# Which queue issues the last stores, and one unit's channel sums four steps later, in a streaming encoder layer

## The chip, the cores and the metric

The kernel runs on one core of a Trainium2 chip. TensorE (PE in the profile) multiplies matrices, with its weight loads shown as PEld; VectorE (DVE), ScalarE (ACT) and GpSimd (POOL) compute on vectors, and SyncE (SP) only issues transfers. SP, ACT and POOL can each issue DMA transfers from their own queue; an instruction in such a queue waits until the one before it has been issued. The metric is the device time of one execution in microseconds.

## The reference

One layer of an encoder processes 512 new frames of one stream (prompt) and 64 frames of a running stream (sample) with 512 cached frames. Everything is float32:

```python
proj = rmsnorm(x, g_norm1) @ w_in               # 2048 -> 6144
q, k, v, gb, gc, hc = split(proj)               # 6 x 1024
q = rmsnorm(q by head, g_q); k = rmsnorm(k by head, g_k)   # 8 heads x 128
o_attn = stick_breaking(q, k, v)                # causal attention
o_conv = gb * conv3_causal(gc * hc)
x = x + concat(rmsnorm(o_attn), rmsnorm(o_conv)) @ w_out
h2 = rmsnorm(x, g_norm2)
x = x + (silu(h2 @ w_gate) * (h2 @ w_up)) @ w_down   # hidden width 5632
```

It returns x for both streams, and the new rows of k, v and of the convolution's state. The two streams are processed together as 576 columns (frames), in two halves of 288; the first half holds prompt frames 0 to 287, the second prompt frames 288 to 511 and the 64 sample frames.

## The kernel before

Each large product is cut into units. A unit is a 256 x 256-blocked strip of weights times the frames, done as a two-by-two block product with seven multiplications in place of eight (numbered 1 to 7 in the code, `run(n, p_)`); each float32 operand is split into a high and a low part, and three matmuls make one full product. A whole multiplication has eight groups of three matmuls. Between groups, `pipe.tick()` counts one **step**, and work that was spawned with a delay is put into the program when its step comes. A unit yields four output blocks, called (c, i): c is the column block of 128 channels, i the half of the frames.

The kernel's stages are: the input stage with the first projection units (to about 100 us), the rest of the input projection (units -22 to -1, to about 570 us), attention and the output projection with it (to about 855 us), gate and up units, and down units, of which the last ones are issued between 1800 us and the end. The order of PE's instructions is written out everywhere. In the down stage the order on ACT, DVE, SP and POOL is written out too (`manual_schedule`); in the projection stage a planner orders these four engines, following what PE's order and the data allow.

**Channel sums.** A unit of kind "qk" gives a head's queries (c = 0) and keys (c = 1). When a block is finished, `a_done` (lines 885 to 907) adds and scales it into a tile E, squares it, and splits the squares into a high and a low part, `s2` (lines 903, 904 on ACT, 905 on DVE). It then spawns `normed` (line 844). That waits a number of steps and issues two matmuls with a matrix of ones, `channel_sums` (lines 283 and 284: the high part, then the low part), four activations on ACT (849 to 852) and three vector operations, and when both halves are done a store of the tile on SP. Key tiles go on to `tokens`, which transposes and stores them. The second qk unit is unit -18 (4 - NA, where NA is 22): the fifth in the list of input units. Its four blocks finish after the multiplications 2, 5, 3 and 4, so `normed` runs four times for it.

**The last stores.** Finished blocks of the down stage are stored in one of two ways. For all units but the last, `store_blocks` transposes a block on DVE (line 1607) and stores it from SP in four pieces (line 1613), with two more for the sample frames if the block is of the second half (line 1615). For the last unit, `store_y` transposes on PE (line 1644), copies with ACT (lines 1647 and 1653), and then stores: a block of the first half by one transfer from SP (line 1656) and one from POOL; a block of the second half by a 64 KB transfer from SP (line 1635), a 48 KB and a 16 KB transfer of the next 128 frames (lines 1635 and 1637) and one from POOL. The last unit's blocks finish in the order (0,0), (1,1), (1,0), (0,1).

The framework that builds the program gives the transfers of SP and ACT eight completion counters, handed out in one rotation over both queues in the order in which its planner places the transfers. A transfer waits on its queue until the counter's last holder has landed. POOL's transfers have eight counters of their own.

Of the kernel before, what the change touches and what calls it, by code (L numbers as in the profile page):

```python
# [16 lines left out]
P = 128  # L17
# [41 lines left out]
NA = len(HEADS_A)  # L59
# [43 lines left out]
def tile_hybrid_stream_step(  # L103
# [6 lines left out]
    nc = tc.nc  # L110
# [30 lines left out]
    def misc(name):  # L141
        return ps_z.tile([P, 512], F32, tag="misc", name=name, bufs=2)
# [13 lines left out]
    NU = len(gu)  # L156
# [110 lines left out]
    def col(name, i=0):  # L267
        return vec[:, rows[name] + i : rows[name] + i + 1]
# [12 lines left out]
    def channel_sums(src_hi, src_lo, a, b, name):  # L281
        ps = misc(name)[:, : b - a]
        mm(ps, oner, src_hi, start=True, stop=False)
        mm(ps, oner, src_lo, start=False, stop=True)
        return ps
# [343 lines left out]
    def hl_tile(name):  # L629
        return tmp.tile([P, 2, HALF], F32, tag="hl", name=name, bufs=3).rearrange("p i t -> p (i t)")  # L630
# [211 lines left out]
        return ((a, min(b, TP), 0),) + (((TP, b, 2),) if b > TP else ())  # L842

    def normed(n, h, c, a, b, s2, E):
        yield 12 if n == -2 else 20
        ms = ss = channel_sums(s2[:, 0], s2[:, 1], a, b, "ss")
        yt = hl_tile("yt")
        y, t = yt[:, :HALF], yt[:, HALF:]
        nc.scalar.activation(out=ms, in_=ss, func=AF.Identity, scale=1.0 / P, bias=epsc)
        nc.scalar.activation(out=y, in_=ms, func=AF.Ln)  # L850
        nc.scalar.activation(out=y, in_=y, func=AF.Exp, scale=-0.5)
        nc.scalar.activation(out=t, in_=y, func=AF.Square)
        nc.vector.scalar_tensor_tensor(out=t, in0=t, scalar=-0.5, in1=ms, op0=ALU.mult, op1=ALU.mult)
        nc.vector.scalar_tensor_tensor(out=t, in0=t, scalar=1.5, in1=y, op0=ALU.add, op1=ALU.mult)
        nc.vector.scalar_tensor_tensor(out=E[:, a:b], in0=E[:, a:b], scalar=col("gk") if c else gqs, in1=t,
                                       op0=ALU.mult, op1=ALU.mult)
        seen[n, c] = seen.get((n, c), 0) + 1
        if seen[n, c] == 2:
            nc.sync.dma_start(out=qk_dram[h, c], in_=E)
            if c:  # L860
                pipe.spawn((last_tokens if n == -2 else tokens)(E, kp[:, h, :], ks[:, h, :], None, 11 if n == -2 else 20))
# [25 lines left out]
    def a_done(n, c, i, ps, part):  # L887
        kind, g = UNITS[n][:2]
        a, b = HALVES[i]
        if kind in ("v", "qk"):  # L890
            if (n, c) not in etile:
                etile[n, c] = (lpool.tile([P, UW - 2], F32, tag=f"c{n + 2}", name="E2")[:, :T]
                               if n > -3 and c == 0 else e_tile(f"E{n}"))
            E = etile[n, c]
            bank = ps
            if part is not None:
                nc.vector.tensor_tensor(out=E[:, a:b], in0=ps, in1=part, op=ALU.add)
                ps = E[:, a:b]
            nc.vector.tensor_tensor(out=E[:, a:b], in0=ps, in1=R1[:, a:b], op=ALU.mult)
            if kind == "qk":  # L900
                sq = hl_tile("sq")[:, :HALF] if c == i == 1 else bank
                s2 = tmp.tile([P, 2, HALF], F32R, tag="hl", name="s2", bufs=3)
                nc.scalar.activation(out=sq, in_=E[:, a:b], func=AF.Square)
                nc.scalar.copy(out=s2[:, 0], in_=sq)
                nc.vector.tensor_tensor(out=s2[:, 1], in0=sq, in1=s2[:, 0].bitcast(F32), op=ALU.subtract)
                pipe.spawn(normed(n, g, c, a, b, s2, E))
                return
            seen[n, c] = seen.get((n, c), 0) + 1
            if seen[n, c] == 2:
                h = 2 * g + c  # L910
                pipe.spawn((last_tokens if n == -1 else tokens)(E, vp[:, h, :], vs[:, h, :], v_dram[h], 3 if n == -1 else 7))
            return
# [631 lines left out]
    for d, v in visits.items():  # L1544
        n = next(a for a, b in zip(v, v[1:]) if a >= NGU + 10 and b >= a + 4)
# [51 lines left out]
    def store_blocks(n, c, i):  # L1597
        d = UNITS[n][1]
        src, c0, f0 = acc[d, c, i], (2 * d + c) * P, HALVES[i][0]
        n_p = min(HALF, TP - f0)  # L1600

        def work():
            yield 9
            if not spare:
                spare.extend(down["pool"].tile([P, HALF], F32, tag=f"ob{k}", name="ob") for k in range(2))
            ob = spare.pop(0)
            nc.vector.transpose(out=ob, in_=src)
            spare.append(src)
            yield 5
            for k in range(P // BK):  # L1610
                rows = ob[k * BK : (k + 1) * BK, :n_p].rearrange("j (t c) -> j t c", c=BK)
                cg = slice(c0 + k * BK, c0 + (k + 1) * BK)
                nc.sync.dma_start(out=yp[f0 : f0 + n_p, cg].rearrange("(t j) c -> j t c", j=BK), in_=rows)
            for a in range(n_p, HALF, BK):
                nc.sync.dma_start(out=ys[a - n_p : a - n_p + BK, c0 : c0 + P].rearrange("j (g c) -> g j c", c=BK),
                                  in_=ob[:, a : a + BK])

        pipe.spawn(work())
# [3 lines left out]
    def store_y(n, c, i):  # L1622
        if n < NU - 1:
            store_blocks(n, c, i)
            return

        d = UNITS[n][1]
        src, cs, f0 = acc[d, c, i], slice((2 * d + c) * P, (2 * d + c + 1) * P), HALVES[i][0]
        r = HALF - 2 * P

        def put(f, ap, queue=nc.sync):

            rows, n_p = ap.shape[0], max(min(TP - f, ap.shape[0]), 0)
            if n_p:
                queue.dma_start(out=yp[f : f + n_p, cs], in_=ap[:n_p])
            if n_p < rows:
                queue.dma_start(out=ys[f + n_p - TP : f + rows - TP, cs], in_=ap[n_p:])

        def work():
            yield 9  # L1640
            po = misc("pot")[:, : 3 * P]
            for q in range(3):
                w = min(P, HALF - q * P)
                nc.tensor.transpose(po[:w, q * P : (q + 1) * P], src[:, q * P : q * P + w], ident)
            yield 3
            ob = src[:, : 2 * P].rearrange("p (i c) -> p i c", c=P)
            nc.scalar.copy(out=ob, in_=po[:, : 2 * P].rearrange("p (i c) -> p i c", c=P))
            if len(rests) % 2 == 0:
                rests.append(spare.pop(0))
            else:  # L1650
                rests.append(rests[-1])
            obs = rests[-1][:r, : P] if len(rests) % 2 else rests[-1][:r, P : 2 * P]
            nc.scalar.copy(out=obs, in_=po[:r, 2 * P :])
            yield 4
            if i == 0:
                nc.sync.dma_start(out=yp[: 2 * P, cs].rearrange("(i p) c -> p i c", p=P), in_=ob)
            else:
                put(f0, ob[:, 0, :])
                put(f0 + P, ob[:, 1, :], nc.scalar if n == NU - 1 else nc.sync)
            put(f0 + 2 * P, obs, nc.gpsimd if n == NU - 1 else nc.sync)  # L1660

        pipe.spawn(work())


# [80 lines left out]
```

## Time and profile before

| | |
|---|---|
| median of three runs | 2339.37 us (2337.11 to 2339.61) |
| the profiled execution | 2339.12 us |
| its span, first to last instruction | 2337.4 us |
| PE busy | 2316.1 us, 99% of the span |
| DVE, ACT, POOL busy | 84%, 52%, 13% |
| DMA | 368.58 MB, mean 158 GB/s |
| granted PE clock, mean | 0.998 |

A row of a timeline gives the start, the duration, the engine, the line of the kernel, the operation and what it writes and reads; "x4" means four merged instructions, and brackets give idle time of the engine before it with what ended it. An engine's name with a q is its queue (SPq, ACTq): there the issue of a transfer is shown, not the transfer. A row of waits says who waited for whom, and gives total time, number of times and the longest.

### The profile page before, as it was taken

What the parts mean: (1) busy time and instruction counts of PE and PEld (TensorE: products, weight loads), DVE (VectorE), ACT (ScalarE), POOL (GpSimd) and SP (SyncE); (2) the same over time, 40 slices, a digit from 0 to 9 for tenths busy, and PEclk for the clock granted to TensorE, in tenths of its full rate; (3) what the DMA queues carried; (4) which work ended last, traced back from release to release, by engine and by line L of the source; (5) the groups of instructions that cost most, each with busy time, mean ns of one, the idle gap of its engine ahead of it and who ended that gap; (6) DMA issues with size and microseconds to landing.
All of it is one profiled execution on the core that took longest, in us unless ns stands there. A gap on an engine that the chain in (4) does not pass through costs nothing.

```text
span 2337.4 us, 43553 instructions
## 1 busy us (share of the span) xinstructions
PE 2316.1 (99%) x17432; PEld 2306.9 (99%) x17432; DVE 1954.1 (84%) x2871; ACT 1221.6 (52%) x2170; POOL 300.6 (13%) x374
## 2 busy tenths in 40 slices
PE   9999999999999999999999999999999999999997
PEld 9999999999999999999999999999999999999997
DVE  8889989897777898888888888888888778887896
ACT  8556656456877654444444444444444444444443
POOL 0211121110332320000000000000000002431222
PEclk9999999999999999999999999999999999999999
DMA  8434343546743454543444444444444936875653
GB/s 271 139 113 129 91 142 110 142 134 206 197 137 118 163 190 126 159 152 121 154 142 136 154 129 149 143 139 150 130 148 140 361 115 225 227 217 188 208 133 80
DMA packets 533771, 368.58 MB, mean 158 GB/s; under 512 B 70278, under 2 KB 518016, under 8 KB 533568
## 3 DMA queue, kind: packets, MB, share of 16 engines
q1 hardware_dynamic: 526752, 356.32, 48.7%
q0 software_dynamic: 6384, 9.21, 2.2%
q8 instruction: 136, 2.23, 0.4%
q14 instruction: 67, 0.55, 0.1%
q10 hardware_dynamic: 432, 0.27, 0.0%
HBM read 285.52 MB, written 80.23 MB: 156 GB/s over the span
## 4 chain that ended last, share of the span: by engine, by line
PE 92%; DVE 3%; ACT 3%; DMA 1%; issue 1%; POOL 0%; SPq 0%; POOLq 0%; DVEq 0%; ACTq 0%
PE psy L405 45%; PE psw L405 23%; PE psx L405 11%; PE pjo L224 6%; PE pj L691 1%; PE pjz L691 1%; DVE whl L229 1%; PE psv L405 1%; PE pjm L691 1%; DMA raw_a<-in_w_down_dram 0%; ACT ph L228 0%; PE psx L556 0%; ACT whi L176 0%; DMA raw_b<-in_w_down_dram 0%; PE z L1176 0%
## 5 line engine op out<-in xcount | busy, mean ns | idle before, releaser
L229 DVE TENSOR_TENSOR whl<-raw_a,whl 128x1024 fp32r<-128x1024 f32 (+4 forms) x384 | 432.2, 1126 | 54.8 <-ACT whl L228 53.4
L405 PE MATMUL psy<-t,whl 128*128 128x288 f32 x3000 | 447.0, 294 | 0.0
L228 ACT CAST whl<-raw_a 128x1024 fp32r<-128x1024 f32 (+4 forms) x384 | 360.1, 939 | 141.5 <-PE psx L405 46.7
L405 PE MATMUL psy<-h_s,whl 128*128 128x288 f32 x2766 | 416.5, 294 | 0.6 <-ACT part L428 0.6
L405 PEld LDWEIGHTS psy<-t,whl 128*128 128x128 f32 x3000 | 414.3, 188 | 0.0
L405 PE MATMUL psw<-t,whl 128*128 128x288 f32 x2688 | 388.9, 294 | 0.0
L405 PEld LDWEIGHTS psy<-h_s,whl 128*128 128x128 f32 x2766 | 383.1, 188 | 0.9 <-ACT part L428 0.8
L405 PEld LDWEIGHTS psw<-t,whl 128*128 128x128 f32 x2688 | 366.8, 188 | 0.0
L228 ACT CAST whl<-raw_b 128x1024 fp32r<-128x1024 f32 (+5 forms) x234 | 211.3, 905 | 208.1 <-issue 71.6
L229 DVE TENSOR_TENSOR whl<-raw_b,whl 128x1024 fp32r<-128x1024 f32 (+5 forms) x234 | 254.7, 1089 | 74.0 <-ACT whl L228 72.6
L428 ACT COPY part<-psy 128x288 f32<-128x288 f32 x309 | 123.1, 399 | 343.3 <-PE psy L405 340.9
L405 PE MATMUL psx<-h_s,whl 128*128 128x288 f32 x1164 | 170.2, 294 | 0.0
L405 PEld LDWEIGHTS psx<-h_s,whl 128*128 128x128 f32 x1164 | 159.6, 188 | 0.0
L228 ACT CAST whl<-s 128x1024 fp32r<-128x1024 f32 (+5 forms) x103 | 95.3, 925 | 122.6 <-PE psw L405 115.0
L405 PE MATMUL psy<-t12a,whl 128*128 128x288 f32 x1056 | 150.6, 295 | 0.4 <-ACT part L428 0.4
L405 PE MATMUL psw<-t34a,whl 128*128 128x288 f32 x1056 | 150.6, 295 | 0.0
L405 PEld LDWEIGHTS psy<-t12a,whl 128*128 128x128 f32 x1056 | 143.5, 188 | 0.9 <-ACT part L428 0.7
L405 PEld LDWEIGHTS psw<-t34a,whl 128*128 128x128 f32 x1056 | 143.3, 188 | 0.0
L1454 POOL DMA_DIRECT2D hid_dram<-form x7 | 5.2, 739 | 952.1 <-DVE form L229 944.9
L229 DVE TENSOR_TENSOR whl<-s,whl 128x1024 fp32r<-128x1024 f32 (+5 forms) x103 | 110.3, 1071 | 19.9 <-ACT whl L228 19.3
L224 PE MATMUL pjo<-mixc,whi 128*128 128x288 f32 x512 | 119.0, 300 | 0.0
L224 PE MATMUL pjo<-mixa,whi 128*128 128x288 f32 x512 | 102.8, 296 | 0.0
(565 smaller groups left out, 3920.6 us busy)
## 6 DMA issues: line engine op xcount, KB each, us to landing
hid_dram<-form SPq DMA_DIRECT2D x147, 288.0 KB
raw_a<-in_w_in_dram SPq DMA_DIRECT2D x22, 1024.0 KB
raw_b<-in_w_in_dram SPq DMA_DIRECT2D x22, 1024.0 KB
raw_b<-in_w_gate_dram SPq DMA_DIRECT2D x22, 1024.0 KB
raw_b<-in_w_up_dram SPq DMA_DIRECT2D x22, 1024.0 KB
raw_a<-in_w_gate_dram SPq DMA_DIRECT2D x22, 1024.0 KB
raw_a<-in_w_up_dram SPq DMA_DIRECT2D x22, 1024.0 KB
h_s<-hid_dram SPq DMA_DIRECT2D x10, 2016.0 KB
```

The lines of the kernel that those rows point to most:

```text
L224: mm(ps, w_[:, k, csl], x_[:, a:b], start=(k == 0 and n == 0), stop=(k == nk - 1 and n == 2))
L228: cast = nc.scalar.copy(out=hi, in_=src)
L229: (lo_eng or nc.vector).tensor_tensor(out=lo, in0=src, in1=hi.bitcast(F32), op=ALU.subtract)
L405: mm(ps, whl[:, w_, j, :], x_, start=(start and j == 0 and q == 0), stop=(j == len(xs_) - 1 and q == 2), skip_group_check=True)
L428: nc.scalar.copy(out=t, in_=st["y"])
L691: mm(banks_[c][i], w3[:, kt % 8, c * P : (c + 1) * P], t[:, x_, :], start=(kt == 0 and n == 0), stop=(kt == KD - 1 and n == 2))
L1454: q.dma_start(out=hid_dram[fp][2 * n - 2 : 2 * n].rearrange("f p t -> p f t"), in_=t.bitcast(F32))
```

## The change

Two edits. The first takes ACT out of the last unit's stores: the second `put` of a second-half block loses its queue argument and takes the default, SP. It is called for blocks (1,1) and (0,1), and each call makes two transfers (48 KB and 16 KB). The second lets the generator `normed` of unit -18 wait 24 steps instead of 20; all other qk units keep 20, and unit -2 keeps 12.

```diff
     def normed(n, h, c, a, b, s2, E):
-        yield 12 if n == -2 else 20
+        yield 12 if n == -2 else 24 if n == 4 - NA else 20
         ms = ss = channel_sums(s2[:, 0], s2[:, 1], a, b, "ss")
...
             else:
                 put(f0, ob[:, 0, :])
-                put(f0 + P, ob[:, 1, :], nc.scalar if n == NU - 1 else nc.sync)
+                put(f0 + P, ob[:, 1, :])
             put(f0 + 2 * P, obs, nc.gpsimd if n == NU - 1 else nc.sync)
```

## The prediction

> **What bounds the kernel now.** I read the page's busy times first, then PE's waits, then the busy time by stretch at the end, then SP's queue there instruction by instruction.
>
> ```profile
> span 2337.4 us, 43553 instructions
> PE 2316.1 (99%) x17432; PEld 2306.9 (99%) x17432; DVE 1954.1 (84%) x2871; ACT 1221.6 (52%) x2170; POOL 300.6 (13%) x374
> ...
> L229 DVE TENSOR_TENSOR whl<-raw_a,whl 128x1024 fp32r<-128x1024 f32 (+4 forms) x384 | 432.2, 1126 | 54.8 <-ACT whl L228 53.4
> ```
>
> ```profile
> PE psx L556 <- DMA xin<-in_x_prompt_dram: 4.0, 2, 3.7
> ...
> PE psy L405 <- ACT part L428: 1.0, 2, 0.6
> PE ss L284 <- DVE s L905: 0.7, 1, 0.7
> ```
>
> PE is busy for all but 21.3 us of the span. PE's waits (total us, times, longest; the row of line 229, a weight split, is needed below) explain few of these, and one of them is the operation that the second edit moves: line 284, the second matmul of a channel sum. The rest lies at the end:
>
> ```profile
> 2314.20:2325.40 11.20, 9.98 (x76) 9.39 (x75) 4.81 (x10) 3.56 (x11) 3.87 (x5) 1.00 0.05 11
> 2325.40:2337.40 12.00, 0.00 (x0) 0.00 (x0) 0.00 (x0) 0.26 (x2) 1.00 (x2) 0.60 0.36 77
> ```
>
> The columns are length, busy PE, PEld, DVE, ACT, POOL, granted clock, DMA share, GB/s. After 2325.4 the core computes nothing and stores for 12.0 us; in the 11.2 us before that, with results at hand, the DMA engines are 5% busy. SP's queue says why (start, us, instruction):
>
> ```profile
> 2314.12 0.32 SPq L1613 DMA_DIRECT2D out_dram<-acc  x1
> 2325.43 0.32 SPq L1613 DMA_DIRECT2D out_dram<-acc  x1
> ...
> 2326.78 1.13 SPq L1615 DMA_DIRECT2D out_dram<-acc  x2
> 2328.01 1.97 SPq L1613 DMA_DIRECT2D out_dram<-acc  x4
> ...
> 2331.26 1.90 SPq L1613 DMA_DIRECT2D out_dram<-acc  x4
> 2333.26 0.40 SPq L1656 DMA_DIRECT2D out_dram<-acc  x1
> ...
> 2334.27 0.40 SPq L1656 DMA_DIRECT2D out_dram<-acc  x1
> 2334.76 0.42 SPq L1635 DMA_DIRECT2D out_dram<-acc  x1
> SPq L1613 <- DMA out_dram<-acc: 11.2, 2, 11.0
> ```
>
> SP issues the first store of a block at 2314.12 and the second at 2325.43: it waited 11.0 us for a transfer to out_dram. All later stores queue behind it, and the last leaves at 2334.76. So SP's queue, not PE, sets the end.
>
> Whose transfer was it? SP had issued none since 2314.12. The others:
>
> ```profile
> 2323.40 0.37 ACT L1647 COPY acc<-pot 128x256 f32<-128x256 f32 x1 [2.69 <-PE pot L1644]
> ...
> 2323.80 0.34 ACTq L1635 DMA_DIRECT2D out_dram<-acc  x1
> 2324.18 0.44 ACTq L1637 DMA_DIRECT2D out_dram<-acc  x1
> 2324.71 0.37 ACT L1647 COPY acc<-pot 128x256 f32<-128x256 f32 x1 [0.79 <-PE pot L1644]
> ...
> 2325.14 0.36 ACT L1647 COPY acc<-pot 128x256 f32<-128x256 f32 x1
> ...
> 2321.11 0.57 POOL L1635 DMA_DIRECT2D out_dram<-acc  x1
> 2324.22 0.52 POOL L1637 DMA_DIRECT2D out_dram<-acc  x1 [2.55 <-ACT acc L1653]
> 2326.10 0.50 POOL L1637 DMA_DIRECT2D out_dram<-acc  x1
> DMA to landing us min/median/max: 1.7/2.3/2.8
> ```
>
> The last row is the time from issue to landing of line 1635's GpSimd stores. By it GpSimd's store of 2321.11 has landed by 2323.9, and that of 2324.22 not before 2325.9: neither fits 2325.43. ACT's of 2323.80 fits, at 1.6 us. The program says the same: SP's and ACT's transfers take eight completion counters in one rotation, each waiting until its counter's last holder has landed, and SP's stuck store comes next after ACT's first store on that counter. ACT could not issue that one before its block was copied, at 2323.77; so a store whose data had lain ready since about 2314.1 waited for the end of the computation.
>
> **The change, part by part.**
>
> *No store on ACT.* Four stores leave ACT's queue, two for each of the blocks (1,1) and (0,1), and SP gets four. With only SP on the counters, each waits for SP's own transfer eight places back. Eight issues at 0.49 us (2334.27 to 2334.76) are 3.9 us, more than the longest landing above, 2.8 us, so I cost that wait at nothing; a landing beyond 3.9 us would show.
>
> From 2314.12 on, worked out from the intervals of the same queue when it ran freely. A block of six stores takes 2331.26 - 2328.01 = 3.25 us, one of four 2333.26 - 2331.26 = 2.00 us. The data of the last two come from
>
> ```profile
> 2316.01 0.47 DVE L1607 STREAM_TRANSPOSE acc<-acc 128x288 f32<-128x288 f32 x1
> 2318.16 0.47 DVE L1607 STREAM_TRANSPOSE acc<-acc 128x288 f32<-128x288 f32 x1
> ```
>
> so the stuck block ends at 2314.12 + 3.25 = 2317.37, the next at 2320.62, the last at 2322.62; their data are ready at 2316.48 and 2318.63, before their turns. The store of (0,0), ready before GpSimd's at 2321.11, goes at 2322.62 and SP is free at about 2323.12. The next three, of (1,1), wait for the copy that ends at 2323.77. So SP idles 0.7 us: that is the cover of the 16 issues from 2314.6 on, and what they take beyond 0.04 us more each goes to the end. From 2323.80, where ACT started, seven stores follow at 0.50 us: three of (1,1), one of (1,0), three of (0,1), the last at 2326.80. The data of (1,0) (2325.08) and (0,1) (2325.50) are ready ahead of 2325.30 and 2325.80 even by the old times; with ACT's two issues (2323.80 to 2324.62) gone from between its copies, the copy of 2324.71 can come some 0.4 us earlier, but SP's rate hides that. GpSimd keeps its stores. SP's last issue moves from 2334.76 to 2326.80: **-7.96 us**.
>
> What then follows the last issue:
>
> ```profile
> L1741 SPq DRAIN  x3: 7/7/7, 2336.6 to 2336.9; - x3
> L1741 POOLq DRAIN  x3: 40/93/3136, 2326.1 to 2337.1; - x3
> ```
>
> Now 2337.4 - 2334.76 = 2.64 us, kept. GpSimd's own ending is next in line: its drain starts at 2326.1, takes at most 3.14 us, and the closing barrier 0.8 us (2336.6 to 2337.4), so at the old times it would hold the end at 2330.0, and at 2329.4 if its stores come 0.6 us sooner behind an ACT that no longer issues. SP's sum, 2326.80 + 2.64 = 2329.44, stands between. Bounds for this part: -8.3 us (a last transfer of 16 KB that lands 0.3 us sooner than one of 64 KB; an estimate) to -6.7 (all 16 issues at the slowest step of the free stretch, (2328.01 - 2326.78)/2 = 0.62 us: 16 x 0.125 = 2.0 us, less the 0.7 of cover, 1.3; GpSimd's 2330.0 lies inside). I take -7.96, since its terms are intervals of this queue itself.
>
> The Trainium skill, page "DMA: Bandwidth & Descriptors", section "Issuing engines are not separate DMA queues", says that transfers of all issuing engines share the same 16 DMA engines, and that issuing from several saves only the sequencer's time to issue. By that rule alone the change gives up 4 x 0.49 = 1.96 us of saved issuing and wins nothing. No bandwidth is lost or won here, but the rule does not count a completion counter shared between two queues; the 11.0 us row does.
>
> *One unit's channel sums four steps later.* A step is three matmuls. The unit is -18, the second with queries and keys; each of its four sums moves by 12 matmuls.
>
> ```profile
> 177.30 0.45 DVE L905 TENSOR_TENSOR s<-psx,s 128x288 fp32r<-128x288 f32 x1
> 176.78 0.29 PE L283 MATMUL ss<-s,oner 128*128 128x288 f32 x1
> 177.80 0.40 PE L284 MATMUL ss<-s,oner 128*128 128x288 f32 x1 [0.72 <-DVE s L905]
> 178.04 1.35 PE L405 MATMUL psy<-t12a,whl 128*128 128x288 f32 x9
> 179.23 3.37 PE L405 MATMUL psy<-b,whl 128*128 128x288 f32 x24
> ...
> 187.59 0.29 PE L283 MATMUL ss<-s,oner 128*128 128x288 f32 x1
> ...
> 187.85 1.38 PE L405 MATMUL psw<-t34a,whl 128*128 128x288 f32 x9
> ```
>
> The undisturbed sum takes 187.85 - 187.59 = 0.26 us of PE's time, this one 178.04 - 176.78 = 1.26: 1.00 us lost, waiting for the low half, which is there at 177.75. Moved, the sum starts after the product's last nine matmuls, 179.23 - 178.04 = 1.19 us later, at 177.97: 0.2 us to spare. Gain 1.00 us. The other three sums did not wait and cost the same elsewhere. But all four now fall on the end of a product; at two of these ends (products 5 and 6) ACT must also copy the bank that the product after next writes, and the sum's chain on ACT may get ahead of the copy. The nearest row is the wait of line 405 for such a copy, 0.6 us at the longest: twice, 1.2. So this part lies between -1.0 and +0.2; I take **-0.9**, near the end where ACT, which is half idle, takes the copy in time. What is queued behind: the unit's query and key rows go to SP's queue 1.6 us later, and so may weight loads behind them; the waits show no wait of PE for any DMA after the first inputs, and weight splits run four products of 24 matmuls ahead, at 0.13 us a matmul (nine in 1.19) 12.7 us, so nothing is charged. Buffers of the sums' rotating tiles are held 1.6 us longer, covered by the same lead.
>
> **Sum.** 2337.4 - 7.96 - 0.9 = 2328.5 us of span. The profiled run took 2339.12, 1.72 outside the span and 0.25 below the median of 2339.37. 2328.5 + 1.72 + 0.25 = 2330.5.
>
> **Rivals.**
> - *The shift buys nothing, or a copy waits at a product's end* (the second part at 0 to +0.2, with SP's slip of up to 1.3 us beside it): 2331.4 to 2332.9. For it: only 0.2 us to spare.
> - *SP's queue becomes slow*: SP is bound by its issues from 2314 on if they take 0.65 us instead of 0.49, or it waits for landings of its own. The 16 then cost 2.6 us more, less the 0.7 of cover, and the seven behind them 1.1: +3.0, 2333.5. Against it: the free stretch after 2328.01.
> - *The wait stays*, because the transfer waited for is another one. Then SP has four more issues at the end: 2339.37 + 1.96 - 0.9 = 2340.4, slower than before, but within 0.2%. It decides from the point where the wait ends later than 2324.4. Against it: no other transfer fits 2325.43. The rule of the Trainium skill above would put it here.
> - *The other side*: the order on DVE, ACT and SP in the first stage is made by a planner that follows PE's order. If the shift makes it put one vector subtract of line 229, 1.1 us, ahead of a split that PE needs in each of the 17 units that follow, PE waits up to 17 x 1.1 = 19 us: 2349.5. It uses up the gain of 8.9 us from 8.9/17 = 0.52 us a unit, and is slower by 0.2% from 0.8. Against it: PE never waits for a split in that stage now, and the splits lead by products.
>
> **How the numbers follow.** 0.2%, 4.7 us, is about what a measurement here can tell from no change (the three runs spread over 2.5). The forecast 0.70, the idle shift 0.17, the slow queue 0.05, the wait that stays 0.04, the planner 0.04. Faster: 0.70 + 0.17 + 0.04 of the slow queue = 0.91; same: 0.05; slower: 0.04. The range takes in the forecast's bounds with one run's spread (2327.8) and the idle shift and part of the slow queue (2334.0).
>
> **What would show it.** Right: no wait of SP for a transfer in the last 30 us; SP's last issue near 2326 (2326.8 less what PE gained); the stretch without computation 5 us long instead of 12; no wait at line 284. Wrong: a gap in SP's queue before 2323, landings over 3.9 us, or new waits of PE for splits or copies before 570 us.

## The result, and the profile after

The changed kernel takes 2329.3 us (median of six runs, 2327.9 to 2329.95), the kernel before 2338.22 us beside it (six runs, 2337.11 to 2339.61): a ratio of 0.9959, with a 95% interval of 0.9947 to 0.9970. That is 8.9 us less, the difference that the prediction's sum gives (8.86 us), and the time lies inside the range; it is 1.2 us below the predicted 2330.5, because the three runs shown before the change lay 1.15 us above the median of all six.

The waits of PE in the profile after (who waited for whom, total us, times, longest):

```profile
core 0 of [0], span 2327.9 us
...
PE psx L556 <- DMA xin<-in_x_prompt_dram: 3.9, 1, 3.9
...
PE psy L405 <- ACT part L428: 0.6, 1, 0.6
```

The wait of line 284 is gone. So is one of the two waits at line 405, of 0.4 us; that one is no part of the change, and the part on the prediction comes back to it. SP's queue at the end, and all that SP waited for from 2290 us on:

```profile
2314.60 1.13 SPq L1615 DMA_DIRECT2D out_dram<-acc  x2
2315.83 1.88 SPq L1613 DMA_DIRECT2D out_dram<-acc  x4
2317.75 1.13 SPq L1615 DMA_DIRECT2D out_dram<-acc  x2
2318.99 1.92 SPq L1613 DMA_DIRECT2D out_dram<-acc  x4
2321.00 0.40 SPq L1656 DMA_DIRECT2D out_dram<-acc  x1
2322.51 0.83 SPq L1635 DMA_DIRECT2D out_dram<-acc  x2
2323.40 0.41 SPq L1637 DMA_DIRECT2D out_dram<-acc  x1
2323.91 0.39 SPq L1656 DMA_DIRECT2D out_dram<-acc  x1
2324.40 0.92 SPq L1635 DMA_DIRECT2D out_dram<-acc  x2
2325.38 0.42 SPq L1637 DMA_DIRECT2D out_dram<-acc  x1
```

```profile
SPq L1613 <- DVE acc L450: 6.7, 4, 2.9
SPq L1635 <- ACT acc L1653: 1.2, 1, 1.2
SPq L1741 <- PEq L1741: 0.6, 2, 0.5
SPq L1741 <- DMA out_dram<-acc: 0.6, 2, 0.4
SPq L1613 <- DVE raw_a L349: 0.3, 1, 0.3
```

SP no longer waits for a transfer before the closing barrier (line 1741). It has stored every block of the older units by 2321, waits 1.2 us for ACT's copy of block (1,1), and then issues seven stores in a row, the last at 2325.38. That is the order of events that the prediction wrote down, 1.4 us earlier.

The first of the two stretches shown for the kernel before, and the stretch without computation of this one, now read so (length, busy PE, PEld, DVE, ACT, POOL, granted clock, DMA share, GB/s):

```profile
2314.20:2325.40 11.20, 8.70 (x66) 8.11 (x65) 3.49 (x7) 3.19 (x11) 4.88 (x7) 1.00 0.37 76
2324.20:2327.90 3.70, 0.00 (x0) 0.00 (x0) 0.00 (x0) 0.00 (x0) 0.46 (x1) 0.90 0.31 85
```

The DMA engines are 37% busy where they were 5%, since the stores now go out while PE finishes. From the end of the last copy (2323.79) to the end of the span are 4.1 us, where there were 11.7.

One number serves for all runs below: the **tail**, from the end of ACT's copy of block (1,1) (line 1647) to the end of the span. It does not depend on how early PE comes there. Before it is 2337.4 - 2323.77 = 13.6 us, after 2327.9 - 2322.48 = 5.4 us, so 8.2 us less.

### The profile page after: what moved, and what is told of

Read it like the earlier page. It is cut to its first block, busy times and chain, and to the rows that moved or that the text cites. A ratio compares the mean times of both kernels' runs of the same rounds, so it can differ in the third digit from the quotient of the medians.

```text
span 2327.9 us, 43552 instructions
## 1 busy us (share of the span) xinstructions
PE 2315.9 (99%) x17432; PEld 2306.7 (99%) x17432; DVE 1956.4 (84%) x2871; ACT 1221.5 (52%) x2170; POOL 298.1 (13%) x374
## 4 chain that ended last, share of the span: by engine, by line
PE 93%; ACT 3%; DVE 2%; DMA 1%; issue 0%; POOL 0%; SPq 0%; POOLq 0%; ACTq 0%; DVEq 0%
PE psy L405 47%; PE psw L405 23%; PE psx L405 12%; PE pjo L224 6%; PE pj L691 1%; PE pjz L691 1%; PE psv L405 1%; PE pjm L691 1%; DMA raw_a<-in_w_down_dram 0%; ACT ph L228 0%; PE psx L556 0%; ACT whi L176 0%; DVE whl L229 0%; DMA raw_b<-in_w_down_dram 0%; DMA vtok<-v_dram 0%
```

## The experiments

Two theories on the tail. **The shared counter**: a store of SP waits until a store of ACT with the same completion counter has landed, and everything behind it waits too. The rival, **the amount**: ACT's stores as such cost time, by their number, their issue or the queue they use, and taking each of them off wins its share. On the sums: PE waited for an operand that came late, against a wait that belongs to the place of the sum in a product.

### The stores alone

```diff
-        yield 12 if n == -2 else 24 if n == 4 - NA else 20
+        yield 12 if n == -2 else 20
```

against the changed kernel.

> The first edit alone: ACT issues none of the last unit's stores, and unit -18 keeps 20 steps. If the shared counter is the cause, the tail's whole gain is here: 2338.2 - 8.0 = 2330.2 us, no wait of SP for a transfer in the last 30 us, and the wait at line 284 stays at 0.7 to 1.0 us. If the gain of the tail needed the earlier PE of the second edit, this run stays above 2332.

Measured: 2330.84 us (2329.08 to 2332.59, five runs) against 2338.72 for the kernel before on the same chip, ratio 0.9966 (0.9954 to 0.9979), so -7.9 us. The tail is 2329.3 - 2323.88 = 5.4 us, as with both edits, and SP waits for no transfer. The wait of the sum is back:

```profile
PE ss L284 <- DVE s L905: 0.8, 1, 0.8
```

The first edit carries the tail's whole gain and needs nothing of the second.

### The sums alone

```diff
-                put(f0 + P, ob[:, 1, :])
+                put(f0 + P, ob[:, 1, :], nc.scalar if n == NU - 1 else nc.sync)
```

> The second edit alone: unit -18 waits 24 steps, ACT keeps its four stores. The wait at line 284 goes and PE comes 1.0 us earlier; since SP's stuck store waits for ACT's store behind PE's last products, the end comes earlier by the same 1.0 us: 2337.2 us, with SP's wait near 10 us instead of 11. If the end were set by SP alone from 2314 on and not by ACT's store, PE's 1.0 us would be lost and the time would stay at 2338.2.

Measured: 2337.34 us (eleven runs) against 2338.72, ratio 0.9995 (0.9986 to 1.0004). The 1.4 us go the expected way, but the interval includes no change: by time alone this edit is not told from nothing. The trace shows its step: no wait at line 284. SP's wait is still 11.0 us at the longest, the same length and not 10, because the stuck store itself, PE and ACT's store all come earlier together:

```profile
SPq L1613 <- DMA out_dram<-acc: 11.4, 2, 11.0
```

ACT's copy of block (1,1) starts 2.65 us earlier than in the profile before, at 2320.75 against 2323.40; the sum explains 1.0 us of that. The tail is 2334.8 - 2321.12 = 13.7 us, unchanged: an earlier PE brings the end earlier by as much, since ACT's store stands between them.

### One block's stores on ACT: (0,1), then (1,1)

Both start from the changed kernel; `c` is the column block. The first leaves the two stores of (0,1) on ACT, the second those of (1,1).

```diff
-                put(f0 + P, ob[:, 1, :])
+                put(f0 + P, ob[:, 1, :], nc.sync if c else nc.scalar)
```

> Both edits, but the last block to finish, (0,1), keeps its two stores on ACT; (1,1) goes to SP. Shared counter: in the built program ACT's 48 KB store now shares its counter with the fifth store of the block where SP got stuck before (its first of line 1615), so four stores of that block go out freely, then SP waits until ACT's store has landed: about 2323.7 + 1.6 = 2325.3. After it come 2 + 6 + 4 stores (1.2 + 3.25 + 2.0 us) and six more at 0.5, the last at 2334.3, and the end 2.6 later: span 2336.9, 2338.6 us, nothing won although half of ACT's stores are gone. If the number of ACT's stores or their issue time were the cause, half the gain would stay: about 2334.

```diff
-                put(f0 + P, ob[:, 1, :])
+                put(f0 + P, ob[:, 1, :], nc.scalar if c else nc.sync)
```

> Both edits, but block (1,1) keeps its two stores on ACT and (0,1) goes to SP. Shared counter: ACT's first store now shares its counter with the fourth store of the stuck block, so three go out freely and SP then waits until ACT's store of 2322.5 has landed, about 2324.1. After it 1.7 + 3.25 + 2.0 us of stores and six more at 0.5, the last at 2333.6: span 2336.2, 2337.9 us. If the number of ACT's stores were the cause: about 2334.

With (0,1) on ACT, 2338.26 us, ratio 0.9998 (0.9989 to 1.0007); with (1,1) on ACT, 2336.47 us, ratio 0.9991 (0.9982 to 1.0000). Half of ACT's stores are gone in each, and nothing or nearly nothing of the gain is there. SP's wait and its restart, first with (0,1) on ACT:

```profile
SPq L1615 <- DMA out_dram<-acc: 10.9, 1, 10.9
```

```profile
2324.21 0.34 ACTq L1635 DMA_DIRECT2D out_dram<-acc  x1
...
2325.99 0.54 SPq L1615 DMA_DIRECT2D out_dram<-acc  x1
```

and with (1,1) on ACT:

```profile
SPq L1613 <- DMA out_dram<-acc: 10.0, 1, 10.0
```

```profile
2321.83 0.34 ACTq L1635 DMA_DIRECT2D out_dram<-acc  x1
...
2323.43 0.32 SPq L1613 DMA_DIRECT2D out_dram<-acc  x1
```

In the first, the store that gets stuck is one of line 1615, the fifth of its block, as the counters of the built program say; in the second, the last of line 1613, the fourth; before the change it was the second. From the issue of ACT's first store to SP's restart it is 1.78 and 1.60 us here, 1.63 before and 1.62 with the sums alone. The tails are 14.5 and 13.3 us, where 14.4 and 13.7 had been worked out. So the amount of ACT's stores is not the cause: two of them, at the wrong places of the rotation, cost what four did, and the later they are issued, the longer SP stands.

### The four stores to GpSimd, and two of them

Both blocks' stores, and then those of (1,1) alone.

```diff
-                put(f0 + P, ob[:, 1, :])
+                put(f0 + P, ob[:, 1, :], nc.gpsimd)
```

> Both edits, but the four stores go to GpSimd's queue instead of SP's. Shared counter: GpSimd's transfers do not share counters with SP's, so SP is as free as in the changed kernel and its last issue comes 1.7 us earlier, at 2323.7. GpSimd now issues seven at 0.58 us from 2322.6, the last at 2326.1, and its drain of 2.4 us and the barrier of 0.7 follow: span 2329.4, 2331.0 us. So taking the stores off ACT is what wins, and SP as their new place is 1.5 us better than GpSimd. If SP had to be the issuer for the gain, the time would be near 2337.

```diff
-                put(f0 + P, ob[:, 1, :])
+                put(f0 + P, ob[:, 1, :], nc.gpsimd if c else nc.sync)
```

> Both edits, but the two stores of (1,1) go to GpSimd and those of (0,1) to SP. SP then issues five from 2322.5, the last at 2324.7, and would end at 2327.2; GpSimd issues five, the last at 2324.9, and with its drain ends at 2328.3. So 2329.3 to 2330.0 us, no better than the changed kernel, because GpSimd's drain takes over the end. If GpSimd's drain does not hold the end, 2328.6.

Measured: 2329.52 us (ratio 0.9961, 0.9946 to 0.9976) and 2329.36 us (0.9958, 0.9942 to 0.9975). The gain does not need SP as the issuer; it needs ACT's stores off the counters that SP uses. The first came 1.5 us faster than expected. Its tail is 2327.7 - 2321.27 = 6.4 us, 1.0 longer than with SP, for which 1.5 had been worked out: GpSimd's issues follow each other at 0.52 us, not 0.58, and the end comes 2.9 us after the last of them (2324.76 to 2327.7), not 3.3.

```profile
2322.17 1.00 POOL L1637 DMA_DIRECT2D out_dram<-acc  x2
2323.23 1.04 POOL L1635 DMA_DIRECT2D out_dram<-acc  x2
2324.26 1.00 POOL L1637 DMA_DIRECT2D out_dram<-acc  x2
```

But PE came to the end 1.2 us earlier than in the changed kernel's profile, and that hid the rest. Its arrival differs between executions; what made it early here was not followed. The second has a tail of 5.4 us, no better than the change: the end comes 3.3 us after SP's last issue (2324.82 to 2328.1) instead of 2.5, since GpSimd, which issues until 2325.7, now holds it. No version here is faster than the changed kernel by anything that can be measured.

### The sums after 22 and after 16 steps

```diff
-        yield 12 if n == -2 else 24 if n == 4 - NA else 20
+        yield 12 if n == -2 else 22 if n == 4 - NA else 20
```

The second kernel has 16 in place of 22.

> The changed kernel with 22 steps for unit -18 instead of 24. The first sum comes 6 matmuls, 0.79 us, earlier than in the changed kernel, at about 177.2, and the low half of its squares is there at 177.36: a wait at line 284 of 0.1 to 0.2 us is left. If the wait had been caused by the place of the sum inside a product and not by the late operand, it would be either whole (0.7) or nothing.

> The changed kernel with 16 steps for unit -18: the first sum comes 24 matmuls, 3.2 us, earlier than in the changed kernel, 1.6 us earlier than before the change. If PE waits there for the low half of the squares, the wait grows from 0.7 to 1.0 us by 1.6 to 2.3 to 2.6 us, and PE comes later by as much to the end of the stage; other sums of the unit may wait too. If the wait is one for a bank or a copy, it does not grow so.

One execution each, 2329.85 and 2330.75 us. With 22 steps no wait is left where 0.1 to 0.2 was expected; with 16 the wait is 1.5 us, not 2.3 to 2.6:

```profile
175.11 0.40 PE L283 MATMUL ss<-s,oner 128*128 128x288 f32 x1
176.99 0.40 PE L284 MATMUL ss<-s,oner 128*128 128x288 f32 x1 [1.49 <-DVE s L905]
```

The wait does grow when PE comes earlier, so it is one for the operand. It grows too little because the operand was earlier as well: it ends at 176.94 here, against 177.80 in the run with the stores alone. PE comes 1.68 us earlier (175.11 against 176.79), the operand 0.86, the difference is 0.82, and the wait grew by 0.7.

So when is the operand ready? What moves with it stands further up the chain: the third activation of line 968, which scales a convolution block of the unit before. These rows are of the kernel before, then of the sums alone:

```profile
166.49 0.54 ACT L968 ACTIVATE mc<-oc,vec 128x288 fp32r<-128x288 f32 x1 [3.51 <-DMA mixc_dram<-mc]
...
177.30 0.45 DVE L905 TENSOR_TENSOR s<-psx,s 128x288 fp32r<-128x288 f32 x1
```

```profile
164.34 0.54 ACT L968 ACTIVATE mc<-oc,vec 128x288 fp32r<-128x288 f32 x1 [1.25 <-DMA mixc_dram<-mc]
...
175.14 0.45 DVE L905 TENSOR_TENSOR s<-psx,s 128x288 fp32r<-128x288 f32 x1
```

ACT stands idle there until a store of an earlier such block has landed and its buffer is free. VectorE waits for this activation in its turn (line 969, 3.16 us idle in the kernel before) and then works without a pause up to the subtract of line 905, so all of it slides together. The subtract starts 10.80 or 10.81 us after the activation in all ten traces with this order: 166.49 and 177.30 before, 166.11 and 176.91 after, 166.54 and 177.35 with the stores alone, 164.34 and 175.14 with the sums alone, 167.13 and 177.94 with (0,1) on ACT, 166.68 and 177.49 with (1,1) on ACT, 165.44 and 176.24 with four stores on GpSimd, 166.80 and 177.61 with two, 165.80 and 176.61 with 22 steps, 165.69 and 176.49 with 16. What sets PE's wait is thus the landing of a store some 11 us earlier, and that moves by 2.8 us between executions. In the sums-alone execution the operand was ready at 175.59; PE came past the sum's old place at 176.2 (177.76, where the sum ran, less twelve matmuls of 0.13), so with 20 steps it would hardly have waited.

### The mixed-convolution stores of one unit to GpSimd

```diff
-        nc.sync.dma_start(out=mixc_dram[g][:, :, a:b], in_=m.bitcast(F32))
+        (nc.gpsimd if n == 3 - NA else nc.sync).dma_start(out=mixc_dram[g][:, :, a:b], in_=m.bitcast(F32))
```

with 20 steps and the first edit.

> The first edit with 20 steps for unit -18, and the four stores of mixed convolution rows (line 971) of the unit before it issued by GpSimd instead of SP. In the other runs the third activation of line 968 sits idle until such a store has landed, and the late low half follows it 10.8 us later. If that store lands late because it stands behind a 1 MB weight load in SP's queue, it now lands some 2 us after its issue, line 968 starts before 164 and its wait is under 1 us. If the DMA engines are busy with the load whoever issues, line 968 still waits until about 166. The planner also moves the low half two weight splits forward on VectorE here, so the wait at line 284 should be gone in both cases, and says nothing on its own.

This one settles less than it was made for. It took 2333.05 us in one execution. The activation still waits, at 168.55 and again at 172.50, though for 1.1 and 1.2 us instead of 3.5; but VectorE's second half of such a block came 5 us later in the new order, so the two cannot be set side by side. Line 971's stores from GpSimd land so (least, median and longest from issue to landing):

```profile
DMA to landing us min/median/max: 2.5/2.7/7.2
```

The first of the four, issued at 157.01, 1 us behind a 1 MB weight load of SP, took 7.2 us; the other three took 2.5 to 2.8. So a store need not stand in SP's queue to land late. This fits DMA engines that are busy whoever issues, and does not prove it: no run moved the load. What the run does show is a price of reordering this stage:

```profile
PE psy L405 <- ACT part L428: 3.0, 2, 2.2
```

PE waited 3.0 us for copies on ACT, 2.2 us of it in this stage, at one copy that the planner had put behind the squares of unit -18; there the kernel before waited 0.4 us.

## Why the prediction was right

**Who held SP.** Right, and shown: the wait is there in each of the four kernels that leave ACT stores of the last unit, ends 1.6 to 1.8 us after ACT's issue in all of them, moves to another store of the block when the rotation moves, and is gone in every kernel where ACT issues none. The rival in which the wait stays is out.

**The tail's term.** Predicted -7.96 us, measured -7.9 with the edit alone by time, and -8.2 by the tail in the traces. Its pieces: SP idles 1.2 us ahead of block (1,1), predicted 0.7; the last issue comes 2325.38 - 2322.48 = 2.90 us after the copy, predicted 3.03; the end 2.52 us after it, predicted 2.64. The cover of the 16 issues held. No landing stood in the way, eight places back. The 0.3 us by which the lower bound let a smaller last transfer land sooner was worked out from no row; the end came 0.12 us sooner. GpSimd's ending, next in line, did not take over: its drain lasts 2.4 us, not 3.1, and is done at 2326.5, before SP's first drain at 2327.1. That the whole change gave 8.9 us, just the predicted sum, is in part luck: between the two profiled executions it is 9.5 us, 8.2 in the tail and 1.3 in PE's arrival, and the two edits alone gave 7.9 and 1.4.

**The rule on issuing engines.** The Trainium skill, page "DMA: Bandwidth & Descriptors", section "Issuing engines are not separate DMA queues", allows a second issuer only the saving of issue time. The seven stores from block (1,1) on do cost SP 0.48 us apiece (2322.51 to 2325.38), so the trace agrees with that saving; it was bought with a wait of 11.0 us, which the section does not speak of.

**The sums' term.** Predicted -0.9 us. The trace bears out the 1.0 us (1.04 us of PE's time lost at this sum with the stores alone, none after), but with two errors. The place was wrong: the sum runs not at the product's end, after nine more matmuls, but after twelve, three into the next product.

```profile
177.60 0.56 PE L405 MATMUL psy<-b,whl 128*128 128x288 f32 x3
177.99 0.29 PE L283 MATMUL ss<-s,oner 128*128 128x288 f32 x1
178.12 0.29 PE L284 MATMUL ss<-s,oner 128*128 128x288 f32 x1
```

The old place was therefore three matmuls off the middle of a product, as its row with nine matmuls behind it showed. The three further matmuls, 0.4 us, turn the "0.2 us to spare" into 0.6: the operand is ready at 177.36 and the sum starts at 177.99. The other error was to take the operand's time as fixed, while it moves with a store's landing. So the term is a mean over executions that differ, not a constant: the operand was some 2 us earlier in one of them. By time alone it stays unproved.

**The copies at a product's end and the planner.** Neither rival came: PE has no new wait in the projection stage. But the last experiment shows 2.2 us lost to just such a copy from another small reordering, so the rival was a real one, and its price of 0.6 us a copy was too small for that case.

**What is not explained.** PE came to the end 1.3 us earlier in the profile after than before, 1.0 of it from the sum. Another 0.4 is the missing wait at line 405. It hangs on the same late landing, so it is chance: the copy that PE waited for runs on ACT 7.74 us behind the third activation of line 968, both before (166.49 and 174.23) and in the run with (0,1) on ACT (167.13 and 174.87), which has such a wait too. Among the traces with 24 steps PE's arrival differs by up to 1.9 us; that was not followed.

## What to carry to other kernels

Where several queues draw completion counters from one rotation, a transfer whose data come late holds the transfers of another queue whose data are ready: look for an idle queue in front of a ready store, and ask which transfer, of whichever queue, had its counter last. A second issuing engine is only free if its transfers are not the late ones. When PE waits on a late operand, follow the chain up until something moves by the same amount in every trace; here it was a store's landing, 11 us upstream.

## What was not expected of the hardware

A store from ACT of 48 KB had landed 1.6 to 1.8 us after its issue in four kernels, by SP's restart; the DMA engines were 20% busy meanwhile in the kernel before. In the projection stage, behind a 1 MB weight load, ACT waited for the landing of a 288 KB store of SP until 3.6 us after the last such issue in one execution (160.70 to 164.34) and 5.9 us in another (160.59 to 166.49), with the same instructions and issue times that differ by 0.1 us. The DMA engines were wholly busy in the 3.3 us ahead of that issue in both. What makes the spread was not found; it decides how long a sum some 11 us later waits.
